# Moving the block for overflowing experts from behind expert 7 to behind expert 60

## The chip, the core and the metric

The kernel runs on one core of a Trainium2 chip: TensorE (PE, with its weight loads PEld), VectorE (DVE), ScalarE (ACT), GpSimd (POOL) and SyncE (SP). Each engine takes its own instructions in order; they wait for each other through semaphores. Transfers between the chip's memory and on-chip memory run on the core's 16 DMA engines and are issued from the queue of an engine, here nearly all from SP. The metric is device microseconds of one execution; times are the median of several executions. A profile is of one execution, and its span goes from the first to the last instruction.

## The reference, cut to what matters

The input is 256 tokens of width 1024, with 16 learned tokens in front. One layer of two linear-attention mixers (gated DeltaNet and GLA) is followed by a mixture of experts, and the result is normalised:

```
h   = h + hybrid_mixer(rmsnorm(h, norm_mix), ...)
xn  = rmsnorm(h, norm_ffn)
group  = argmax(xn @ w_group + b_group)                  # 8 groups
e1, e2 = top 2 of the 8 experts inside the group         # 64 experts in all
y[t]   = sum over e1, e2 of gate * ((silu(xn @ w1[e]) * (xn @ w3[e])) @ w2[e])
out = rmsnorm(h + y, norm_final)                         # the 16 learned tokens are dropped
```

An expert has w1 and w3 (1024 x 512) and w2 (512 x 1024) in float32, 6.3 MB. Which tokens go to which expert is known only at run time; 512 token places fall on 64 experts.

## The kernel before, in words

The mixer takes the first 400 us or so. Behind it all 64 experts are worked through in order, whatever their number of tokens. An expert has room for 32 tokens (`CAP`). What does not fit is done by a block that runs a loop over lists of overflowing experts, with a number of turns that is known only at run time; this is the function `overflow` (L1370). It reads the number of turns into a register of every engine, and a `tc.If` (L1372) jumps over the loop where it is zero.

**Weights.** The host lays the weights out as `wx[e, part]`: parts 0 and 1 hold w1 and w3 of one half of the 1024 rows each, part 2 holds w2. A part is 2 MB and stands in one buffer of 16 KB per partition: `lateA` to `lateE` and `ring0` to `ring4`. `ring_load` (L172) issues a part from SP's queue (L193); expert 63's parts go as two halves of 1 MB. `ring_more` (L195) issues as many as there are free buffers; `ring_take` (L204) hands a part out for use and puts its buffer back on the free list, and the load of the next part into it waits until PE has read the old one. Each transfer reports on one of eight completion semaphores, which the framework gives out in turn, whatever queue the transfer is issued from; a transfer is issued only when the one before it on the same semaphore has landed.

**One expert** (the loop from L1425 on). `up` (L1313) multiplies the expert's gathered tokens `xg` with parts 0 and 1 into the PSUM bank `h13` (matmuls `h`, 64 of them in the trace). `swiglu` (L1325) makes `sl` on ACT and `hid` on DVE, `turn` (L1332) transposes it on PE and copies it to `hT`, and `down` (L1348) multiplies it with part 2 into the banks `y0` and `y1` (matmuls `y`, 16). `scaled` (L1343) writes the two halves of the result to `ys`: ACT the first 512 columns, DVE the second. `back` (L1367) adds `ys` to the tokens' rows by one-hot matmuls into four PSUM banks `acc` that stay open over all experts (matmuls `acc`, 8). In the program text an expert's `back` stands in the next expert's turn, behind that one's `up` and `swiglu`; the framework's scheduler, which simulates the times of each stretch between branches, sets the order on each engine's queue.

**The tile that holds `ys`.** From expert 4 on `ys` lies in `yy[0]`, a tile of 2048 columns: even experts use the first 1024, odd ones the second (`scratch`, L1358). The block's loop uses the same tile: its 16 transfers of w1 and w3 and its 4 of w2 go from SP into the two halves of `yy[0]` in turn (L1402 to L1416), and its own `ys` into the first half.

```
wo = yy[0][:, 1024 * (k % 2):][:, :1024]                       # in overflow, k from 0 to 7
return [yy[0][:, 1024 * (e % 2) + 512 * i:][:, :512] for i in range(2)]   # scratch(e)
```

**The end.** Behind expert 62 the residual `h` is added to `acc` by 8 matmuls with the identity, and `norm_final` is loaded into the same tile that held `h` (L1482). Expert 63's `down` works by halves; then come the sum of squares, the reciprocal root on POOL, the scaling on DVE and four stores.

`with after(slab_dma)` keeps a load of experts' weights behind the last load of the mixer's weights on SP's queue; it may only name an instruction of the same stretch between branches.

Of the kernel before, what the change touches and what calls it, by code (L numbers as in the profile page):

```python
# [18 lines left out]
P = 128  # L19
D = 1024  # L20
# [6 lines left out]
NE = 64  # L27
# [69 lines left out]
def _body(tc, a, dbg, stop, ctx, nc, V, S, G, PE):  # L97
# [7 lines left out]
    def ts(out, in0, s1, s2, op0, op1=None, eng=None, **kw):  # L105
        e = eng or V
        if op1 is None:
            e.tensor_scalar(out, in0, s1, None, op0=op0, **kw)  # L108
        else:
            e.tensor_scalar(out, in0, s1, s2, op0=op0, op1=op1, **kw)  # L110

    def tt(out, in0, in1, op, eng=None):
        return (eng or V).tensor_tensor(out, in0, in1, op)  # L113
# [10 lines left out]
    def mm(out, lhsT, rhs, start=True, stop=True, **kw):  # L124
        return PE.matmul(out, lhsT, rhs, start=start, stop=stop, **kw)  # L125
# [35 lines left out]
    nload, slab_dma, gathered, gather_after, lead, x_act, x_dve = [0], [None], [None], [None], [None], [None], [None]  # L161

    def after(cell):

        return tc.issue_after(cell[0].ins) if cell[0] is not None else ExitStack()
# [6 lines left out]
    def ring_load(n, count):  # L172

        e, part, hf = n // 6, n // 2 % 3, n % 2
        if e == SPARE // 6:
            part = (0, 2, 1)[part]
        if n == SPARE:
            ring[e, part] = [w2p.tile([P, 2048], F32, name="ys", bufs=1)]
        elif hf == 0 or n == SPARE + 1:
            slot = ring_free.pop(0)  # L180
            ring.setdefault((e, part), []).extend((slot[0].tile([P, 4096], F32, name=slot[1], bufs=1), slot))
        t = ring[e, part][-2 if n != SPARE else 0]
        src = wx[e, part]
        if n == SPARE:
            to, src = t, src[:, 0:2048]
        elif part == 2 and e == NE - 1:
            hs = slice(512 * hf, 512 * hf + 512)
            to, src = t.rearrange("p (j d) -> p j d", j=4)[:, :, hs], src.rearrange("p (j d) -> p j d", j=4)[:, :, hs]
        else:
            hs = slice(2048 * hf, 2048 * (hf + count))  # L190
            to, src = t[:, hs], src[:, hs]
        with after(slab_dma):
            nc.sync.dma_start(to, src)  # L193

    def ring_more(n=6 * NE, whole=True):  # L195
        while n and nload[0] < 6 * NE and (ring_free or (nload[0] % 2 == 1) != (nload[0] == SPARE + 1) or nload[0] == SPARE):
            i = nload[0]
            count = 2 if whole and i % 2 == 0 and i != SPARE and i < 6 * (NE - 1) else 1
            ring_load(i, count)
            nload[0] += count  # L200
            n -= 1

    def ring_take(e, part):
        *spare, t, slot = ring.pop((e, part))  # L204
        ring_free.append(slot)
        return (spare[0], t) if spare else t
# [936 lines left out]
    def rt(shape, name):  # L1143
        return mo.tile(shape, F32, name=name)
# [93 lines left out]
    def overflow_list():  # L1238
        ec, eo = rt([P, 2, 64], "ec"), rt([P, 2, 64], "eo")
        tt(ec, rp, C2("ecode")[:, None, :].to_broadcast([P, 2, 64]), ALU.add)  # L1240
        for i, cd in enumerate((cd1, cd2)):
            tt(eo, oh12[:, :, i], ec, ALU.mult)
            V.tensor_reduce(cd, eo, axis=AX.X, op=ALU.add)
        over = rt([P, 64, 7], "over")
        tt(over, cnt[:, :, None].to_broadcast([P, 64, 7]), C2("steps")[:, None, :].to_broadcast([P, 64, 7]), ALU.is_gt)
        nit = rt([P, 1], "nit")
        V.tensor_reduce(nit, over.rearrange("p a b -> p (a b)"), axis=AX.X, op=ALU.add)
        V.tensor_copy(niti, nit)
        ov = over.rearrange("p a b -> p (a b)")
        tt(ov, ov, C2("icode"), ALU.mult)  # L1250
        V.max(items[:, 0:8], ov)
        V.match_replace(out=ov, in_to_replace=items[:, 0:8], in_values=ov, imm_value=0.0)
        V.max(items[:, 8:16], ov)
        ts(items, items, 1.0, 1.0, ALU.max, ALU.subtract)
        V.tensor_copy(itemi, items)
        ts(itemi, itemi, 3, None, ALU.arith_shift_right)
        ts(items, items, 32.0, None, ALU.mult)
# [5 lines left out]
    def bank(*names):  # L1263
        return [pm.tile([P, 512], F32, name=n) for n in names]
# [18 lines left out]
    def group(g):  # L1283

        es = slice(GR * g, GR * g + GR)
        ohs = w2p.tile([P, 2, GR * CAP], F32, name="ohs")
        orep = w2p.tile([P, 2, GR, P], F32, name="orep", bufs=1)
        with after(gathered):
            for t in range(2):
                late_dve[0] = tt(ohs[:, t].rearrange("p (e s) -> p e s", e=GR), rp[:, t, es][:, :, None].to_broadcast([P, GR, CAP]),  # L1290
                   slots[:, None, :CAP].to_broadcast([P, GR, CAP]), ALU.is_equal)
        XG[g] = w2p.tile([P, KT, GR * CAP], F32, name="xg")
        yield from gather(XG[g], ohs, GR * CAP, *((2, ("y0", "y1", "misc", "y0")) if g == 0 else ()))
        with after(gathered):
            for t in range(2):
                tt(orep[:, t], rp[:, t, es][:, :, None].to_broadcast([P, GR, P]), slots[:, None, :].to_broadcast([P, GR, P]), ALU.is_equal)
        p = pm.tile([P, 512], F32, name="misc")
        for e in range(GR):
            for t in range(2):
                mm(p[:, 2 * e:2 * e + 2], orep[:, t, e], rg[:, t, GR * g + e], start=(t == 0), stop=(t == 1))  # L1300
        SC[g] = w2p.tile([P, GR, 2], F32, name="sc")
        V.tensor_copy(SC[g], p[:, 0:2 * GR].rearrange("p (e c) -> p e c", c=2))
        yield
        for e0 in range(0, GR, 2):
            p = pm.tile([P, 512], F32, name="misc")
            for e in range(2):
                for t in range(2):
                    PE.transpose(p[:, (2 * e + t) * P:(2 * e + t + 1) * P], orep[:, t, e0 + e], ident)
            WOT[g, e0] = w2p.tile([P, 2, 2, P], F32, name="wot", bufs=4)
            act(WOT[g, e0], p.rearrange("p (e t x) -> p e t x", e=2, t=2))  # L1310
            yield
# [53 lines left out]
    def back(out, wot, ys, start, stop):  # L1365
        for t in range(2):
            for hf in range(2):  # L1367
                mm(out[2 * t + hf], wot[:, t], ys[hf], start=start, stop=stop)
# [73 lines left out]
    for e in range(NE):  # L1442
        g, i = divmod(e, GR)
        if i == 0 and e:
            for _ in nxt:
                pass
            nxt = group(g + 1) if g + 1 < NE // GR else iter(())
        a0, a1 = ring_take(e, 0), ring_take(e, 1)
        with after(lead if e == 1 else [None]):
            ph = up(XG[g], (a0, a1), slice(CAP * i, CAP * i + CAP), bank("acc3" if e == 1 else "h13")[0],  # L1450
                    {0: first_group, NE - 1: keep_warm}.get(e))
        hid = swiglu(ph, SC[g][:, i])
        if e == 0:
            nxt = group(1)
        if e == 1:
            acc = bank("acc0", "acc1", "acc2", "acc3")
        if last is not None:
            back(acc, *last, start=(e == 1), stop=False)
        hT = turn(hid)
        for _ in range(2):  # L1460
            next(nxt, None)
        c0 = ring_take(e, 2)
        if e == NE - 1:
            break
        ys = down(hT, c0, SC[g][:, i], scratch(e))
        last = (WOT[g, i // 2 * 2][:, i % 2], ys)
        if e == 1:
            with tc.issue_after(late_dve[0].ins):
                overflow_list()
        if e == OVER:  # L1470
            back(acc, *last, start=False, stop=False)
            last = None
            slab_dma[0] = None
            overflow(acc)
            gathered[0] = None
        ring_more()
        if e == NE - 2:
            for t in range(2):
                for hf in range(2):
                    mm(acc[2 * t + hf], ident, h[:, t, hf * 512:hf * 512 + 512], start=False, stop=False)  # L1480
            nfin = keep.tile([P, 2, D], F32, name="h")[:, 0]
            nc.sync.dma_start(nfin, a["norm_final"][None, :].to_broadcast([P, D]))  # L1482


    py, sc, wot = bank("y0", "misc", "y1", "h13"), SC[g][:, i], WOT[g, i // 2 * 2][:, i % 2]
# [36 lines left out]


GR = 4
OVER = 7
SPARE = 20
WARM = 72
E1 = 0
# [74 lines left out]
```

## Time and profile before

| | us |
|---|---|
| median of 3 runs | 1344.37 (1342.24 to 1346.36) |
| the profiled execution | 1344.17 |
| its span | 1342.4 |
| PE busy | 1179.6 (88% of the span) |
| DVE, ACT, POOL busy | 447.5, 314.6, 92.4 |
| transfers of queue q1 (SP's) | 457.43 MB, 83.4% of 16 engines' span |

The span is 24165 instructions long; it is cut in 40 slices of 33.6 us in the page's second part. A busy share is an average over the mixer, where PE is the busiest, and the experts, where the transfers are.

### The profile page before, as it was taken

Reading aid. Unit: us, or ns where it says so; the run is one execution under the profiler, and the core shown is the slowest. Engines: PE = TensorE matmul, PEld = TensorE weight load, DVE = VectorE, ACT = ScalarE, POOL = GpSimd, SP = SyncE. Lnnn points to the kernel's source line nnn. Section 1 sums busy time; section 2 is a strip of 40 time slices with the busy share of each in tenths; the row PEclk is TensorE's granted clock in tenths of the full one; section 3 lists DMA queues with packets and bytes.
Section 4 is the critical chain, followed back from the end, with each engine's and each line's share of the span. In section 5 each row is a group of like instructions: output and inputs, shape, how many; then the busy total and the mean of one; then the engine's idle time right before and its main releaser. Section 6 shows DMA issues by size and latency. Waiting matters only on the chain.

```text
span 1342.4 us, 24165 instructions
## 1 busy us (share of the span) xinstructions
PE 1179.6 (88%) x10513; PEld 760.3 (57%) x10513; DVE 447.5 (33%) x1007; ACT 314.6 (23%) x681; POOL 92.4 (7%) x163
## 2 busy tenths in 40 slices
PE   9999999999999998898878888788788878878776
PEld 8998999899997454344333434334343434334323
DVE  6689787656665222111110101111110111111101
ACT  5575565365441111101000000100000001010101
POOL 1016214502000000000000000000000000000000
PEclk8999999999999999999998898989998998999999
DMA  7633332333997999899999999999999999999995
GB/s 267 217 111 110 113 117 90 126 110 117 369 372 306 427 428 426 366 427 427 427 426 428 428 427 426 426 429 427 425 428 429 427 425 428 428 428 425 428 425 226
DMA packets 46287, 459.53 MB, mean 342 GB/s; under 512 B 5441, under 2 KB 5697, under 8 KB 20450
## 3 DMA queue, kind: packets, MB, share of 16 engines
q1 hardware_dynamic: 45890, 457.43, 83.4%
q8 instruction: 83, 1.36, 0.4%
q10 hardware_dynamic: 288, 0.52, 0.1%
q14 instruction: 26, 0.21, 0.0%
HBM read 456.89 MB, written 1.05 MB: 341 GB/s over the span
## 4 chain that ended last, share of the span: by engine, by line
DMA 44%; PE 15%; ACT 1%; DVE 1%; issue 0%; DVEq 0%; POOL 0%; SPq 0%
DMA ring<-wx 15%; DMA lateB<-wx 9%; DMA lateA<-wx 9%; DMA lateE<-wx 6%; PE acc L125 5%; PE h L125 4%; DMA lateC<-wx 3%; DMA lateD<-wx 3%; PE y L125 3%; PE misc L125 2%; ACT ys L116 1%; ACT sl L116 0%; DVE hid L1329 0%; PE misc L1334 0%; DVE hT L1336 0%
## 5 line engine op out<-in xcount | busy, mean ns | idle before, releaser
L125 PE MATMUL acc<-ys,wot 128*128 128x512 f32 x480 | 226.8, 615 | 27.6 <-ACT ys L116 26.9
L125 PEld LDWEIGHTS acc<-ys,wot 128*128 128x128 f32 x480 | 88.6, 195 | 155.6 <-issue 92.3
L1329 DVE SCALAR_TENSOR_TENSOR hid<-h,sc,sl 128x128 f32<-128x128 f32 x63 | 22.1, 350 | 451.6 <-ACT sl L116 451.6
L125 PE MATMUL ip<-xh,lateD 128*128 128x256 f32 (+2 forms) x784 | 162.3, 297 | 0.0
L116 ACT ACTIVATE sl<-h,sc 128x128 f32<-128x128 f32 x63 | 23.2, 368 | 481.5 <-PE h L125 476.1
L125 PE MATMUL h<-ring,xg 128*32 128x256 f32 x2048 | 124.9, 382 | 6.5 <-DMA ring<-wx 6.3
L125 PEld LDWEIGHTS ip<-xh,lateD 128*128 128x128 f32 x784 | 128.8, 194 | 1.9 <-issue 0.3
L125 PE MATMUL ip<-xl,lateD 128*128 128x256 f32 (+2 forms) x392 | 115.6, 295 | 0.0
L116 ACT ACTIVATE ys<-y,sc 128x512 f32<-128x512 f32 (+1 forms) x61 | 41.5, 680 | 280.4 <-PE y L125 280.4
L125 PEld LDWEIGHTS h<-ring,xg 128*32 128x32 f32 x2048 | 62.5, 110 | 74.7 <-issue 25.6
L108 DVE TENSOR_SCALAR ys<-y,sc 128x512 f32<-128x512 f32 x59 | 44.3, 750 | 167.7 <-PE y L125 167.7
L113 DVE TENSOR_TENSOR lateD<-slab,lateD 128x1024 fp32r<-128x1024 f32 x64 | 80.9, 1264 | 30.7 <-ACT lateD L116 29.4
L116 ACT ACTIVATE lateD<-slab 128x1024 fp32r<-128x1024 f32 x64 | 67.7, 1058 | 57.0 <-PE ip L125 54.7
L125 PE MATMUL y<-ring,hT 128*32 128x512 f32 x496 | 68.2, 667 | 14.4 <-DMA ring<-wx 14.0
L125 PEld LDWEIGHTS ip<-xl,lateD 128*128 128x128 f32 x392 | 75.8, 194 | 1.1 <-issue 0.3
L125 PEld LDWEIGHTS misc<-ohs,h 128*128 128x128 f32 x488 | 56.8, 191 | 22.2 <-issue 12.1
L125 PE MATMUL misc<-ohs,h 128*128 128x128 f32 x488 | 62.7, 281 | 6.4 <-DVE hT L1336 6.4
L156 POOL TENSOR_TENSOR rss<-rss,c 128x1 f32<-128x1 f32 x2 | 1.1, 556 | 925.2 <-DVE rss L103 925.2
L1334 PE MATMUL misc<-c,hid 128*128 128x128 f32 x64 | 20.8, 324 | 49.0 <-DVE hid L1329 49.0
L125 PE MATMUL ip<-xl,wh 128*128 128x256 f32 (+2 forms) x192 | 57.3, 298 | 0.0
L125 PE MATMUL ip<-xh,wh 128*128 128x256 f32 (+2 forms) x192 | 56.8, 296 | 0.0
L125 PE MATMUL ip<-xh,wl 128*128 128x256 f32 (+2 forms) x192 | 56.1, 292 | 0.0
(480 smaller groups left out, 1643.0 us busy)
## 6 DMA issues: line engine op xcount, KB each, us to landing
ring<-wx SPq DMA_DIRECT2D x90, 2048.0 KB, 39.2
lateA<-wx SPq DMA_DIRECT2D x19, 2048.0 KB, 39.2
lateD<-wx SPq DMA_DIRECT2D x19, 2048.0 KB, 39.2
slab<-w_in SPq DMA_DIRECT2D x72, 512.0 KB, 3.7
lateC<-wx SPq DMA_DIRECT2D x18, 2048.0 KB, 39.2
lateB<-wx SPq DMA_DIRECT2D x18, 2048.0 KB, 39.2
lateE<-wx SPq DMA_DIRECT2D x17, 2048.0 KB, 39.1
ring<-wx SPq DMA_DIRECT2D x12, 1024.0 KB, 8.9
```

What stands on the lines that cost most here:

```text
L108: e.tensor_scalar(out, in0, s1, None, op0=op0, **kw)
L113: return (eng or V).tensor_tensor(out, in0, in1, op)
L116: return S.activation(out, in_, func, **kw)
L125: return PE.matmul(out, lhsT, rhs, start=start, stop=stop, **kw)
L156: G.tensor_tensor(out, x, C(name, n)[:, :w], ALU.pow)
L1329: late_dve[0] = V.scalar_tensor_tensor(hid, ph[:, P:256], sc[:, 0:1], sl, op0=ALU.mult, op1=ALU.mult)
L1334: PE.transpose(p[:, 0:P], hid, ident)
```

## The change

The block is called behind expert 60 and no longer behind expert 7. `ring_more` is called ahead of it, so that at expert 60 all 384 halves are issued before it, and an assertion says so. `slab_dma` is cleared behind every expert and not only where the block stands, and the load of `norm_final` is issued from ACT's queue (`S`) and not from SP's.

```diff
+        ring_more()
         if e == OVER:
+            assert nload[0] == 6 * NE
             back(acc, *last, start=False, stop=False)
             last = None
-            slab_dma[0] = None
             overflow(acc)
             gathered[0] = None
-        ring_more()
+        slab_dma[0] = None
         if e == NE - 2:
             for t in range(2):
                 for hf in range(2):
                     mm(acc[2 * t + hf], ident, h[:, t, hf * 512:hf * 512 + 512], start=False, stop=False)
             nfin = keep.tile([P, 2, D], F32, name="h")[:, 0]
-            nc.sync.dma_start(nfin, a["norm_final"][None, :].to_broadcast([P, D]))
+            S.dma_start(nfin, a["norm_final"][None, :].to_broadcast([P, D]))
...
-OVER = 7
+OVER = 60
```

## Rows read from the trace of the kernel before

**Rows 1.** The page's second part: GB/s in 40 slices of the span.

```profile
GB/s 267 217 111 110 113 117 90 126 110 117 369 372 306 427 428 426 366 427 427 427 426 428 428 427 426 426 429 427 425 428 429 427 425 428 428 428 425 428 425 226
```

**Rows 2.** The page's fourth part: the chain of waits, shares of the span by engine.

```profile
DMA 44%; PE 15%; ACT 1%; DVE 1%; issue 0%; DVEq 0%; POOL 0%; SPq 0%
```

**Rows 3.** Windows: us, engines' busy time (instructions), granted clock, DMA share, GB/s.

```profile
540.00:545.00 5.00, 4.76 (x37) 2.89 (x38) 0.92 (x2) 1.18 (x2) 0.00 (x0) 1.00 0.37 98
545.00:550.00 5.00, 5.00 (x44) 2.34 (x46) 0.00 (x0) 0.00 (x0) 0.00 (x0) 1.00 0.86 357
```

**Rows 4.** Waits of SP's queue: us in total, times, longest.

```profile
SPq L193 <- DMA ring<-wx: 339.9, 75, 5.9
...
SPq L1372 <- SPq L1372: 28.7, 7, 6.2
```

**Rows 5.** Line 1372 on SP, whole span and 538 to 544: ns, first and last start.

```profile
L1372 SPq EVENT_SEMAPHORE  x9: 17/17/17, 515.0 to 543.4; - x9
...
L1372 SPq EVENT_SEMAPHORE  x2: 17/17/17, 543.3 to 543.4; - x2
```

**Rows 6.** Timeline, 519 to 545 us: start, us, engine, line [idle before <- releaser].

```profile
519.04 1.93 PE L125 MATMUL h<-lateC,xg 128*32 128x256 f32 x32 [0.41 <-PEq L1372]
...
541.71 1.94 PE L125 MATMUL y<-ring,hT 128*32 128x512 f32 x16
...
543.54 0.34 SPq L193 DMA_DIRECT2D lateC<-wx  x1
...
543.74 0.69 ACT L116 ACTIVATE ys<-y,sc 128x512 f32<-128x512 f32 x1 [5.05 <-PE y L125]
543.78 0.75 DVE L108 TENSOR_SCALAR ys<-y,sc 128x512 f32<-128x512 f32 x1 [1.79 <-PE y L125]
```

**Rows 7.** Timeline of SP's queue, 1258 to 1310 us: the last loads.

```profile
1258.59 0.33 SPq L193 DMA_DIRECT2D lateB<-wx  x1
1263.47 0.33 SPq L193 DMA_DIRECT2D ring<-wx  x1
...
1278.13 16.16 SPq L193 DMA_DIRECT2D ring<-wx  x4
1298.90 10.31 SPq L193 DMA_DIRECT2D lateE<-wx  x2
1309.32 1.84 SPq L1482 DMA_DIRECT2D h<-norm_final  x1
```

**Rows 8.** Tile lateE, 1290 to 1342 us: its loads' starts, and issue to landing.

```profile
L193 SPq DMA_DIRECT2D lateE<-wx x2: 655/3061/5467, 1298.9 to 1303.7; - x2
...
DMA to landing us min/median/max: 25.1/26.2/27.3
```

**Rows 9.** Timeline, 1298 to 1313 us: expert 61's end and expert 62.

```profile
1298.97 1.95 PE L125 MATMUL y<-lateB,hT 128*32 128x512 f32 x16 [1.85 <-DMA lateB<-wx]
1301.02 0.75 DVE L108 TENSOR_SCALAR ys<-y,sc 128x512 f32<-128x512 f32 x1 [3.57 <-PE y L125]
1301.04 0.69 ACT L116 ACTIVATE ys<-y,sc 128x512 f32<-128x512 f32 x1 [4.68 <-PE y L125]
1301.78 1.99 PE L125 MATMUL acc<-ys,wot 128*128 128x512 f32 x4 [0.86 <-ACT ys L116]
...
1308.85 1.93 PE L125 MATMUL h<-ring,xg 128*32 128x256 f32 x32
...
1312.57 0.37 ACT L116 ACTIVATE sl<-h,sc 128x128 f32<-128x128 f32 x1 [10.85 <-PE h L125]
```

**Rows 10.** Windows, 1284 to 1286 us.

```profile
1284.00:1286.00 2.00, 1.70 (x9) 0.52 (x13) 0.00 (x0) 0.00 (x0) 0.00 (x0) 0.50 0.96 410
```

**Rows 11.** Timeline of PE at expert 60's last product.

```profile
1284.30 3.35 PE L125 MATMUL y<-ring,hT 128*32 128x512 f32 x16 [3.06 <-DMA ring<-wx]
```

**Rows 12.** Windows, 15 to 20 us.

```profile
15.00:20.00 5.00, 5.00 (x22) 4.63 (x21) 3.35 (x5) 2.38 (x3) 2.50 (x3) 0.50 0.84 293
```

## Prediction

> **What bounds the kernel now.** I read the page's second part first, for where the transfers are at their ceiling. From the fourteenth slice on the kernel moves 425 to 429 GB/s in every slice but two: one at 366, which runs from 537 to 570 us, and the last [rows 1]. So from about 435 us the experts go at the pace at which 64 × 6.3 MB of weights arrive, one 2 MB load in 4.9 us, 14.7 us for an expert. The chain of waits agrees: 44% of the span is DMA, 15% PE, nearly nothing else [rows 2]. Its PE pieces between 519 and 655 us only say that a freed buffer let a load be issued; the queue was never empty there after 550. Time is therefore won where the queue runs dry before the end, or where the tail behind the last loads gets shorter.
>
> The slice at 366 is the place of the block. Cut in 5 us stretches, it shows 98 and then 357 GB/s between 540 and 550 us [rows 3]. The waits of SP's queue name the line: L1372, the `If`, 28.7 us in 7 waits, the longest 6.2 [rows 4]. Its nine semaphore instructions run from 515.0 to 543.4 us, the last two at 543.3 and 543.4 [rows 5], and the next load leaves SP at 543.54 [rows 6]. The reader is to see what the block costs when it is not taken (no instruction of its body is in the trace). Transfers report on eight completion semaphores in turn. The path that skips the body must raise each of them by what the body's 20 transfers would have added, and SP does that one after the other, waiting before each for the load under way on that semaphore. So SP stands until everything issued has landed, and no load is behind it.
>
> **The change part by part.** *The block leaves expert 7.* SP goes on issuing. The loads lost there: (427−98)/427 × 5 + (427−357)/427 × 5 = 3.85 + 0.82 = 4.7 us; from the slice, (427−366)/427 × 33.6 = 4.8. I take 4.8, bounds 4.5 and 5. At 515 us some six loads were still under way (28.3 us of waits at 4.9 each), and the three that expert 7's freed buffers allow would have joined them, so without the block the queue does not run dry, and every later landing comes 4.8 us earlier.
>
> *The block arrives behind expert 60.* By then SP has issued all loads, so nothing of theirs stands behind the wait. What stands behind it is less visible. The body loads its weights into `yy[0]`, the two halves in turn, and behind the block ACT and DVE write their scaled results `ys` into the same tile: odd experts into the second half. These copies must wait for the body's last transfers into their part of it, that is for semaphores that on the skipped path SP raises. The body's 15th and 16th transfers (w1 and w3 of k=7) went to the second half's two quarters; with eight semaphores in turn they fall on those of the second last and the very last load issued ahead of the block. In the program of the kernel before, ACT's copy of expert 9 waits for the first, DVE's for the second, and both for that of the 20th. There it was hidden: the last load's semaphore was raised at 543.3 [rows 5], and expert 9's `y` matmuls, begun at 541.71, ended only at 543.65; the copies started at 543.74 and 543.78 [rows 6]. The cover was 0.4 us.
>
> At expert 60 it is gone. The first expert behind the block is 61, odd. Its copies now start at 1301.04 and 1301.02 [rows 9], 4.8 us earlier without the gap: 1296.2. But the last loads ahead of the block are then the halves of expert 63's w2. SP issues 8 loads ahead: each leaves as the one eight before it lands (1258.59, 1263.47, and so on) [rows 7]. The two halves (tile lateE) leave at 1298.9 and 1303.7 and land 27.3 and 25.1 us later [rows 8], at 1326.2 and 1328.8; this way round, because the other would land the second at 1331.0 behind norm_final, which was issued after it on that queue. Less 4.8: 1321.4 and 1324.0. So ACT's copy of expert 61 can start at 1321.4 and not at 1296.2.
>
> *What that holds up.* On ACT the later `sl` and `ys`; on PE, whose queue is in order, the `acc` matmuls of expert 61, and behind them all of 62 and 63. PE's path from there now has no DMA wait in it: `acc` of 61 with the residual begins at 1301.78, expert 62 at 1308.85, and the span ends at 1342.4 [rows 9], so 40.6 us from that `acc` to the end. The copy takes 0.69 [rows 9], with 0.1 around it: `acc` begins at 1322.2. Its first eight matmuls use ACT's half and last 3.5 us, so that DVE's half (1324.0 + 0.75 + 0.1 = 1324.9) is there in time.
>
> *The clock behind the wait.* PE stands 26 us. Before expert 60's `y` it stood 3.06 us, and the sixteen matmuls took 3.35 us [rows 11] where expert 61's took 1.95 [rows 9]: 1.4 us lost, with a granted clock of 0.50 [rows 10], the lower level, 1.2 GHz. At the start of the kernel the half clock lasted longer, still 0.50 from 15 to 20 us [rows 12]. Bounds: 0, and 5 us (some 10 us at half pace, an estimate from that start). I take 1.5, by the nearest row.
>
> *The branch itself.* At expert 7 PE lost 0.41 us in front of the first `h` matmul [rows 6]. Behind expert 60 this lies ahead of a wait of 25 us: nothing either way.
>
> *norm_final from ACT.* It must follow the residual's matmuls, which read the tile that it overwrites; they come after the wait, when no load is left. SP needed 1.84 us for this issue [rows 7]; on ACT that lies beside 3.7 us of PE between the residual and `sl`. Nothing; 1.8 if that cover fails. Moving `ring_more` and clearing `slab_dma` change the order of no load that I can name: nothing, bounds ±0.5.
>
> *Sum.* 1322.2 + 40.6 + 1.5 = 1364.3 us of span; 1.8 us lie around the span in the profiled execution (1344.17 against 1342.4): **1366 us**. Against that execution it is −4.8 + 25.2 + 1.5 = +21.9, where 25.2 is the distance from 1296.2 to 1321.4. The median of the runs, 1344.37, is 0.2 above it, so the figure holds for the median too.
>
> **Rivals.** *A: the order on PE is another.* If the matmuls of expert 62 are queued ahead of expert 61's `acc`, they run inside the wait: 3.7 us and about 1 of `sl` and `hid` drop out of the tail, 1361. For it: the program text has them in that order. Against it: in all late experts the queue has `acc` first, and the landing of weights that this order reckons with does not change. 0.13.
>
> *B: only the last transfer into the half counts.* The copies then wait for the 20th transfer's semaphore alone, the fourth in SP's turn, on which the second half of expert 63's first load lands. Four 4.9 us loads behind the one that expert 61's `y` waited for until 1298.97 [rows 9], that is 1318.5, less 4.8: 1313.7. `acc` at 1314.5, + 40.6 + 1.5 + 1.8: 1358. Against it: the wait on the other two is in the program before. 0.05.
>
> *C: the copies do not wait; norm_final does.* Then `acc` of 61 begins 4.8 us early, but norm_final's issue sits in ACT's queue ahead of expert 62's `sl` and needs the fifth semaphore, free only after SP has raised it at about 1316.5, where `sl` is due at 1312.57 − 4.8 = 1307.8 [rows 9]; with its own 1.84 us ACT is free 10.5 us late: 1344.2 − 4.8 + 10.5 = 1350. On SP the trace shows such holding: 339.9 us of SP's waits are for a load to land before the next is issued [rows 4]. The Trainium skill, "DMA: Bandwidth & Descriptors", section "Anatomy of one DMA", says that DMA engines do not wait on semaphores and any such wait happens on the issuing sequencer before dispatch; by that rule moving the transfer to ACT moves its wait into ACT's in-order queue, and SP's rows here agree. 0.04.
>
> *D: faster.* Neither wait is there, or both are met: the body's writes count as done for every engine that did not run it. Then only the gap goes: 1344.2 − 4.8 = 1339.4, and the branch's 0.4 us fall into the 1.85 us for which PE waits at expert 61's `y` [rows 9]. It decides at the copies of expert 61: if they start near 1296, it is this. For it: in the trace before no copy is held. Against it: that those were held for 0.4 us less than they needed anyway. 0.07.
>
> That the block costs SP nothing where it leaves (no gain) is excluded by the two stretches at 98 and 357 GB/s.
>
> **How the numbers follow.** The forecast's own case has 0.71: 1362 to 1371, from the bounds of the clock (0 to 5) and of the gap. With A it holds 0.84. The range 1358 to 1371 takes in A and the edge of B; C, D and most of B are left out. Faster by over 0.3%: D, 0.07. Within 0.3% (about 4 us, what repeated runs of this kernel can tell from no change): 0.02, a C that is half covered. Slower: 0.91.
>
> **What would show it.** Right: no slice below 420 GB/s between 450 and 1300 us; all `L1372` semaphore instructions of SP between about 1299 and 1324, 4.9 and then 2.5 us apart; `ys` of expert 61 on ACT at about 1321 and on DVE at about 1324, with some 25 us of idle PE before its `acc`; a half clock for a few us behind it; 40 to 43 us from that `acc` to the end. Wrong: copies at about 1296 (D, or C if `sl` of 62 is late behind the DMA issue on ACT), a load that still waits in SP behind the branch, or `h` matmuls of expert 62 inside the wait (A).

## The result, and the profile after

The changed kernel takes 1363.22 us (median of 5 runs, 1362.15 to 1364.38), the kernel before 1342.24 over its five: ratio 1.0166, 95% interval 1.0138 to 1.0194. It is slower by 21 us by the two medians and by 22 us by the ratio. The profiled execution took 1363.22 us with a span of 1360.4.

The transfers did gain. This is the page's second part of the changed kernel, GB/s in 40 slices of 34.0 us; the slice at 366 of [rows 1] is gone, nothing between the 14th and the 38th slice is below 424, and the last two slices hold 258 and 47: the last load lands 41 us ahead of the end.

```profile
GB/s 276 205 122 110 119 104 120 111 109 187 379 315 374 428 427 426 426 429 425 428 426 428 428 425 429 425 428 428 424 428 427 426 428 426 428 426 427 426 258 47
```

The two stretches of [rows 3], in windows of the changed kernel (us, busy time and count of PE, PEld, DVE, ACT, POOL, granted clock, DMA share, GB/s):

```profile
540.00:545.00 5.00, 4.10 (x66) 2.12 (x65) 0.35 (x1) 0.37 (x1) 0.00 (x0) 1.00 1.00 424
545.00:550.00 5.00, 3.76 (x23) 1.57 (x24) 1.04 (x2) 1.28 (x2) 0.00 (x0) 1.00 1.00 419
```

What that won is lost behind expert 60. The waits between 1290 us and the end (engine and line, what was waited for: us in total, times, longest) have two rows that the kernel before has not:

```profile
DVE ys L108 <- SPq L1372: 25.9, 1, 25.9
...
ACT ys L116 <- SPq L1372: 24.4, 1, 24.4
...
PE acc L125 <- ACT ys L116: 22.6, 2, 21.8
```

Line 1372 in the changed kernel, all engines (count: ns min/median/max, first and last start):

```profile
L1372 SPq EVENT_SEMAPHORE  x9: 17/17/17, 1300.5 to 1319.4; - x9
...
L1372 PEldq COMPARE_BRANCH  x1: 6508/6508/6508, 1278.7 to 1278.7; - x1
```

And the timeline from expert 60's `acc` to expert 62's `sl` (start, us, engine, line, tiles, idle before and what ended it), against [rows 9]:

```profile
1278.01 3.70 PE L125 MATMUL acc<-ys,wot 128*128 128x512 f32 x8 [0.82 <-ACTq L1372]
1285.58 3.64 PE L125 MATMUL h<-ring,xg 128*32 128x256 f32 x32 [3.88 <-PEq L1372]
...
1293.69 2.18 PE L125 MATMUL y<-lateB,hT 128*32 128x512 f32 x16 [0.43 <-issue]
1316.91 0.69 ACT L116 ACTIVATE ys<-y,sc 128x512 f32<-128x512 f32 x1 [24.42 <-SPq L1372]
1317.65 3.78 PE L125 MATMUL acc<-ys,wot 128*128 128x512 f32 x4 [21.77 <-ACT ys L116]
1319.53 0.75 DVE L108 TENSOR_SCALAR ys<-y,sc 128x512 f32<-128x512 f32 x1 [25.94 <-SPq L1372]
...
1326.89 1.93 PE L125 MATMUL h<-ring,xg 128*32 128x256 f32 x32
1327.00 0.38 ACTq L1483 DMA_DIRECT2D h<-norm_final  x1
...
1330.67 0.37 ACT L116 ACTIVATE sl<-h,sc 128x128 f32<-128x128 f32 x1 [13.07 <-PE h L125]
```

Expert 61's `y` ends at 1295.87. The copies start at 1316.91 and 1319.53, each 0.1 us behind one of SP's last two semaphore instructions (1316.8 and 1319.4). Line 1372 on SP from 1315 to 1320 us, and the tile lateE, whose two loads are the last:

```profile
L1372 SPq EVENT_SEMAPHORE  x2: 17/17/17, 1316.8 to 1319.4; - x2
```

```profile
L193 SPq DMA_DIRECT2D lateE<-wx x2: 662/3090/5519, 1289.6 to 1294.5; - x2
...
DMA to landing us min/median/max: 24.9/26.0/27.2
```

1289.6 + 27.2 = 1316.8 and 1294.5 + 24.9 = 1319.4. Between the end of `y` and the first `acc` at 1317.65 PE stood 21.8 us.

The chain of waits no longer helps here: it follows a wait back to an instruction that did work, and a semaphore that SP raises is none, so it stops at the copy and sums to 2% PE:

```profile
PE 2%; DVE 0%; ACT 0%; issue 0%; DVEq 0%; POOL 0%; ACTq 0%
```

**Taking the executions apart.** Single executions of one kernel differ by up to 13 us here (1331.66 to 1344.71 for own_tile), and the profiles show that some of it arises before the experts: the first load of experts' weights left at 337.06 us in the profile before and at 331.97 in this one. The granted clock of TensorE goes with it, taken over the first 330 us: the rows of the kernel before, of the changed kernel and of `fill_longer` below, whose first load left at 338.47, in this order:

```profile
0.00:330.00 330.00, 321.44 (x3061) 300.95 (x3062) 242.66 (x560) 186.48 (x445) 89.88 (x159) 0.97 0.43 138
```

```profile
0.00:330.00 330.00, 321.24 (x3104) 301.02 (x3105) 244.97 (x566) 188.44 (x449) 90.61 (x160) 0.99 0.44 140
```

```profile
0.00:330.00 330.00, 322.81 (x3049) 302.06 (x3050) 242.25 (x559) 184.94 (x441) 87.86 (x159) 0.96 0.44 138
```

So each profile is cut at two SP issues, the first load of experts' weights and the first half of expert 63's w2 (lateE, [rows 7]); the two stretches behind the first cut are what the kernels can differ in:

| kernel | ratio to before (95%) | first load, us | first load to lateE | lateE to the end |
|---|---|---|---|---|
| before | | 337.06 | 961.8 | 43.5 |
| changed | 1.0166 (1.0138 to 1.0194) | 331.97 | 957.7 | 70.8 |
| own_tile | 0.9975 (0.9955 to 0.9996) | 330.00 | 958.0 | 43.6 |
| other_half | 1.0090 (1.0059 to 1.0121) | 330.36 | 957.9 | 60.7 |
| no_block | 0.9973 (0.9957 to 0.9990) | 331.63 | 958.1 | 43.3 |
| early_wait | 0.9983 (0.9961 to 1.0005) | 335.48 | 961.3 | 44.8 |
| norm_from_sp | one execution | 333.19 | 957.9 | 71.1 |
| fill_wait | 1.0154 (1.0121 to 1.0186) | 329.78 | 958.0 | 66.3 |
| fill_longer | 1.0108 (1.0073 to 1.0143) | 338.47 | 957.7 | 64.0 |

The change is −4.1 in the first stretch and +27.3 in the second: +23.2 us. The spans of these two executions differ by only 18.0, because the changed one reached its first load 5.1 us earlier; the medians, 21.0 apart, lie between. Each stretch is from one execution of a kernel, but the first one agrees closely: 957.7 to 958.1 us in the seven kernels without the block behind expert 7, 961.3 and 961.8 in the two with it.

### The profile page after: what moved, and what is told of

The parts are those of the page before. It is cut to its first block, busy times and chain, and to the rows that moved or that the text cites. A ratio compares the mean times of both kernels' runs of the same rounds, so it can differ in the third digit from the quotient of the medians.

```text
span 1360.4 us, 24163 instructions
## 1 busy us (share of the span) xinstructions
PE 1186.3 (87%) x10513; PEld 762.3 (56%) x10513; DVE 447.1 (33%) x1007; ACT 314.3 (23%) x681; POOL 92.4 (7%) x163
## 5 line engine op out<-in xcount | busy, mean ns | idle before, releaser
L125 PE MATMUL acc<-ys,wot 128*128 128x512 f32 x480 | 231.5, 626 | 47.0 <-ACT ys L116 45.5
L125 PE MATMUL h<-ring,xg 128*32 128x256 f32 x2048 | 126.9, 386 | 10.1 <-DMA ring<-wx 6.0
L113 DVE TENSOR_TENSOR lateD<-slab,lateD 128x1024 fp32r<-128x1024 f32 x64 | 80.8, 1263 | 28.8 <-ACT lateD L116 27.2
L125 PEld LDWEIGHTS misc<-ohs,h 128*128 128x128 f32 x488 | 56.8, 191 | 22.6 <-issue 12.1
```

## The experiments

**own_tile: the copies write a tile that the block does not load into.**

```diff
-        if e <= SPARE // 6:
+        if e <= SPARE // 6 or e > OVER:
             return [rtp.tile([P, 512], F32, name="hT", bufs=2) for _ in range(2)]
```

> The changed kernel with one difference: the experts behind the block keep their scaled results in tiles of their own, which the block's body does not load into. Theory (the copies of expert 61 wait for semaphores that SP raises when the last loads have landed, because they write the tile of the body's transfers): the copies start right behind the y matmuls, near 1296 us in the changed kernel's time and not at 1316.9 and 1319.5; SP's semaphore instructions still run until about 1319; the acc matmuls start 21 us earlier and 2 us of slow clock go: 1340 us, 1338 to 1343. Rival 1 (the block itself costs it at this place: the branch, or SP standing, whatever tile the copies write): unchanged, 1363. Rival 2 (norm_final's issue on ACT takes over the wait and holds sl of expert 62): sl is late by up to 9 us, 1349.

Measured: 1337.53 us (12 runs) against 1340.39 (30 runs). Timeline and line 1372 of this kernel:

```profile
1288.03 2.24 PE L125 MATMUL y<-lateB,hT 128*32 128x512 f32 x16 [0.52 <-DMA lateB<-wx]
1290.33 0.69 ACT L116 ACTIVATE hT<-y,sc 128x512 f32<-128x512 f32 x1 [3.59 <-PE y L125]
1290.37 0.75 DVE L108 TENSOR_SCALAR hT<-y,sc 128x512 f32<-128x512 f32 x1 [2.54 <-PE y L125]
1291.06 1.98 PE L125 MATMUL acc<-hT,wot 128*128 128x512 f32 x4 [0.80 <-ACT hT L116]
...
1299.07 0.38 ACTq L1483 DMA_DIRECT2D h<-norm_final  x1
...
1301.90 0.37 ACT L116 ACTIVATE sl<-h,sc 128x128 f32<-128x128 f32 x1 [10.89 <-PE h L125]
```

```profile
L1372 SPq EVENT_SEMAPHORE  x9: 17/17/17, 1298.9 to 1319.0; - x9
```

SP raises its semaphores as late as in the changed kernel, and no copy waits: they start with the end of `y`, and from lateE to the end 27 us come back. The loss is the tile that the body's transfers would write, not the place of the block. To share a tile with the body is not enough: the `hT` of the pool `rtp`, which these copies now write, is also the name of the tiles in which the body would build its one-hot matrices, with DVE and without a transfer, and that holds nobody here. Rival 2 falls as well: ACT issues norm_final at 1299.07, and `sl` of expert 62 follows its `h` at 1301.90, held by PE alone. The branch is not in the way either: PE still waits 0.52 us for expert 61's weights behind it. This kernel is faster than both, by 0.25% than the one before, with an interval that just excludes no change; the first stretch of the table gives 3.8 us. The forecast of 1338 to 1343 was missed by 0.5 us on the low side; in this series the kernel before is itself 1.9 us faster than in the one above (1340.39 against 1342.24). The earlier `ring_more`, the cleared `slab_dma` and norm_final from ACT are all in this kernel, and its two stretches are those of no_block to within 0.3 us: together they cost nothing.

**other_half: the halves exchanged for the experts behind the block.**

```diff
-        return [yy[0][:, 1024 * (e % 2) + 512 * i:][:, :512] for i in range(2)]
+        return [yy[0][:, 1024 * ((e + (e > OVER)) % 2) + 512 * i:][:, :512] for i in range(2)]
```

> The changed kernel with the two halves of the tile exchanged for the experts behind the block: expert 61 writes the first half, 62 the second. Theory: the last transfer of the body into the first half is its 19th, on the third semaphore in SP's turn, raised at about 1306.8 us; both copies of expert 61 start there, 10 us earlier than ACT's in the changed kernel; expert 62's copies, which now wait for the last two (1316.8 and 1319.4), are due at about 1324 and wait no longer. 1353 us, 1351 to 1355. Rival 1 (the copies wait until SP is through the block, whatever the semaphore): unchanged, 1363. Rival 2 (any copy into this tile is free if it is not the second half): 1340.

Measured: 1351.70 us; from lateE to the end 10.1 us less than the changed kernel. Its timeline, experts 61 and 62:

```profile
1305.50 0.69 ACT L116 ACTIVATE ys<-y,sc 128x512 f32<-128x512 f32 x1 [19.35 <-SPq L1372]
1305.52 0.75 DVE L108 TENSOR_SCALAR ys<-y,sc 128x512 f32<-128x512 f32 x1 [18.27 <-SPq L1372]
...
1322.85 0.69 ACT L116 ACTIVATE ys<-y,sc 128x512 f32<-128x512 f32 x1 [3.18 <-PE y L125]
1322.89 0.75 DVE L108 TENSOR_SCALAR ys<-y,sc 128x512 f32<-128x512 f32 x1 [2.12 <-PE y L125]
```

SP's semaphore instructions of line 1372 from 1303 to 1306 us:

```profile
L1372 SPq EVENT_SEMAPHORE  x2: 17/17/17, 1303.0 to 1305.4; - x2
```

Both copies now start 0.1 us behind the one at 1305.4, 12.7 us ahead of SP's last (1318.2 in this execution), and expert 62's, which belong to the last two, wait for PE alone. So each copy waits for the semaphore of the transfer that would have written its columns, and not until SP is through.

**no_block: the kernel before without the block** (the loop for overflowing experts is left out).

```diff
-OVER = 7
+OVER = NE
```

> The kernel before without the block (the loop for overflowing experts is left out; with this input it makes no turn). Theory (behind expert 7 the block costs the 4.8 us in which the transfers run dry, and nothing else that reaches the end): no slice below 420 GB/s between 450 and 1290 us, and 0.9964 of the kernel before, 1337.5 us for a median of 1342.2. Rival (the end is set by PE's path from 519 to 655 us, which the chain of waits lists, and the gap was filled anyway): the same as before, 1342.

Measured: ratio 0.9973; first load to lateE 958.1 us against 961.8, lateE to the end 43.3 against 43.5. Its GB/s by slice:

```profile
GB/s 276 211 121 117 114 111 96 128 112 126 373 349 340 427 428 426 428 426 427 427 427 427 427 426 427 429 427 428 426 427 428 427 426 427 427 427 427 428 426 211
```

The gap was on the path, and the PE pieces that the chain lists between 519 and 655 us were not. At the last load it is worth 3.7 us here, 4.1 in the changed kernel, and not the 4.8 that the rates give. The rates themselves are right: in the 50 us from 200 us behind the first load on, which hold the gap, the kernel before moved 387 GB/s and the changed one 426, which is 39/426 × 50 = 4.6 us.

```profile
537.06:587.06 50.00, 42.97 (x380) 21.24 (x376) 8.73 (x19) 5.30 (x10) 0.00 (x0) 1.00 0.93 387
```

```profile
531.97:581.97 50.00, 44.47 (x401) 21.50 (x400) 8.08 (x17) 5.04 (x9) 0.00 (x0) 0.97 1.00 426
```

**early_wait: the same wait behind expert 7.** The kernel before, block behind expert 7, with the same edit, so that expert 8 has to wait for the last two semaphores.

```diff
-        return [yy[0][:, 1024 * (e % 2) + 512 * i:][:, :512] for i in range(2)]
+        return [yy[0][:, 1024 * ((e + (e > OVER)) % 2) + 512 * i:][:, :512] for i in range(2)]
```

> The kernel before, block behind expert 7, with the halves exchanged for the experts behind it: expert 8 writes the second half, and its copies have to wait for the last two semaphores, raised at about 543.3 us, where they were due at 529.4. Theory: the same wait as in the changed kernel, 14 us, stands in the trace, but PE has over 50 experts in which each of its turns is 1.5 us or more shorter than three loads, and catches up before the end; the transfers keep enough free buffers: the same time as before within 0.3%. Rival (a wait of this kind costs its length wherever it stands): 14 us slower, 1356.

Measured: ratio 0.9983, no difference. Timeline of this kernel, a later window, and its PE at expert 61's last product:

```profile
536.20 0.69 ACT L116 ACTIVATE ys<-y,sc 128x512 f32<-128x512 f32 x1 [13.24 <-SPq L1372]
...
536.94 3.78 PE L125 MATMUL acc<-ys,wot 128*128 128x512 f32 x4 [6.92 <-ACT ys L116]
...
541.10 0.75 DVE L108 TENSOR_SCALAR ys<-y,sc 128x512 f32<-128x512 f32 x1 [14.20 <-SPq L1372]
```

```profile
560.00:600.00 40.00, 34.47 (x308) 16.77 (x306) 7.17 (x15) 3.76 (x7) 0.00 (x0) 1.00 1.01 428
```

```profile
1296.80 3.30 PE L125 MATMUL y<-lateB,hT 128*32 128x512 f32 x16 [1.85 <-DMA lateB<-wx]
```

Waits of 13.2 and 14.2 us stand in the trace, of which PE stands 6.9 us in front of `acc`, and they cost nothing that the interval shows: the loads are back at 428 GB/s by 560 us, and PE has caught up over the 55 experts that follow, since at expert 61 it waits 1.85 us for weights as in [rows 9]. The 1.3 us by which this execution is longer behind lateE are this `y`, for the most part at the lower clock level (0.57 from 1297 to 1300 us): 3.30 us and not 1.95. Behind expert 60 there is nothing left to catch up in.

**norm_from_sp: the last part of the change undone.**

```diff
-            S.dma_start(nfin, a["norm_final"][None, :].to_broadcast([P, D]))
+            nc.sync.dma_start(nfin, a["norm_final"][None, :].to_broadcast([P, D]))
```

> The changed kernel with norm_final issued from SP's queue again, behind the raising of the semaphores. Theory (this part of the change is worth nothing): it leaves SP at about 1327 us behind the residual's matmuls, lands 25 us before it is needed at 1354; 1363 us, from 1360 to 1366. Rival (it was moved because SP issues it too late): the scaling at the end waits for it, and the span is longer by the time from 1354 to its landing.

Measured: 1364.0 us in one execution, 71.1 us from lateE to the end against 70.8. SP issues it here:

```profile
1328.88 0.35 SPq L1483 DMA_DIRECT2D h<-norm_final  x1
```

It lands 3.7 us later, 23.5 us before the first scaling at 1356.12. This part is worth nothing, as far as one execution shows.

**fill_wait and fill_longer: PE kept busy inside the wait.** `ylast` is the last `y` matmul that was written.

```diff
+        if e == OVER + 1:
+            fill = pm.tile([P, 512], F32, name="misc")
+            with tc.issue_after(ylast[0].ins):
+                for _ in range(320):                # 400 in fill_longer
+                    mm(fill[:, 0:P], zero, zero)
```

> The changed kernel with 320 small matmuls of zeros on PE between expert 61's y and its acc, some 19 us of work that nobody reads, inside the wait. Theory (behind the wait PE runs at half clock for some us because it stood): the acc matmuls and the residual's take 7.1 us to expert 62's first h and not 9.2, at a granted clock of 1.00; the copies start as before at about 1317 and 1319.5; 1361 us, 2 less than the changed kernel. Rival (the slow clock there comes from the branch or from the transfers, not from the standing): 9.2 us again, 1363.

Measured: 1361.17 us. The edit did two things: with the matmuls of zeros in the queue the scheduler put expert 62's `h` ahead of expert 61's `acc`, inside the wait (the order of rival A), and PE then stood 4.3 us before the copies came:

```profile
1315.86 2.08 PE L125 MATMUL acc<-ys,wot 128*128 128x512 f32 x2 [4.28 <-ACT ys L116]
1317.73 0.75 DVE L108 TENSOR_SCALAR ys<-y,sc 128x512 f32<-128x512 f32 x1 [29.92 <-SPq L1372]
...
1318.53 5.49 PE L125 MATMUL acc<-ys,wot 128*128 128x512 f32 x6 [0.60 <-DVE ys L108]
...
1329.87 1.94 PE L125 MATMUL y<-lateD,hT 128*32 128x512 f32 x16
```

From lateE to the end it is 4.5 us shorter than the changed kernel, which is about rival A's price and not the clock's: the granted clock was 0.50 again. So the forecast time of 1361 was met by luck, not by the reason given for it, and this kernel says nothing on its own about the clock; fill_longer was made of it.

> As fill_wait, with 400 matmuls in place of 320, so that PE works up to the moment at which the copies come and does not stand 4.3 us ahead of them. In both, expert 62's h matmuls run inside the wait. Theory (the slow clock behind the wait comes from the standing): from expert 61's first acc to expert 62's y at a granted clock of 1.00 and in some 9 us, the wait for DVE's copy included, and not in 14.0 us as in fill_wait with 0.50 over its first 8; 4 us less than fill_wait, 1357. Rival (the slow clock comes from something else at that place): 14 us again, 1361.

Measured: 1357.20 us. PE worked until ACT's copy was there, and 1.1 us beyond it:

```profile
1323.93 0.69 ACT L116 ACTIVATE ys<-y,sc 128x512 f32<-128x512 f32 x1 [29.53 <-SPq L1372]
...
1325.70 1.13 PE L125 MATMUL acc<-ys,wot 128*128 128x512 f32 x2
1326.54 0.75 DVE L108 TENSOR_SCALAR ys<-y,sc 128x512 f32<-128x512 f32 x1 [30.90 <-SPq L1372]
...
1327.34 2.84 PE L125 MATMUL acc<-ys,wot 128*128 128x512 f32 x6 [0.52 <-DVE ys L108]
...
1335.84 1.94 PE L125 MATMUL y<-lateD,hT 128*32 128x512 f32 x16
```

The same eight `acc` matmuls and the residual's eight up to expert 62's `y`: 10.1 us and not 14.0. The windows behind the copies, of fill_wait and of fill_longer:

```profile
1320.00:1322.00 2.00, 2.00 (x3) 0.67 (x2) 0.00 (x0) 0.00 (x0) 0.00 (x0) 0.50 0.00 0
```

```profile
1328.00:1330.00 2.00, 2.00 (x6) 0.83 (x5) 0.00 (x0) 0.00 (x0) 0.00 (x0) 1.00 0.00 0
```

At 1.2 GHz in the one, at 2.4 in the other. The two kernels differ only by 80 matmuls of zeros, and so in whether PE stood 4.3 us before the copies: the slow clock comes from the standing. Its price is not the whole 3.9 us: 1.0 of it is that in fill_longer PE was still busy with expert 62's `h` when ACT's copy ended (1324.62), so that the stretch begins later against the loads. From DVE's copy, which is tied to the last load in both, to `y` it is 12.1 and 9.3 us: 2.8 us for the clock. Measured from the issue of lateE, DVE's copy comes 0.4 us later in fill_longer (30.4 against 30.0); that leaves 2.4, and the table has 2.3. The medians, 1361.2 and 1357.2, lie further apart, but their intervals overlap (1.0121 to 1.0186 and 1.0073 to 1.0143), so the gain on the whole time is not shown by itself.

## Why the prediction was right, point by point

**The bound and the gap.** Right in kind: the block behind expert 7 held SP until every load had landed, and moving it let the transfers run on. The term was sized at 4.8 us. The rates confirm it where the gap is (4.6), but the issue of the last load came only 3.7 (no_block) to 4.1 us (changed, by the two cuts) earlier. Where the rest goes between the gap and that issue stays open: outside the gap both run at 427 GB/s in every window that I compared.

**The wait that takes its place.** Right, and decided by other_half: the copies of expert 61 wait for the second last and the last load of all, through semaphores that SP raises on the skipped path. Forecast for ACT's copy 1321.4, measured 1316.91, which is 1322.0 if the 5.1 us of the earlier start are put back: 0.6 late, as the gap was worth less.

**What it holds up.** `acc` to the end was forecast as 40.6 + 1.5 = 42.1 us; it was 1360.4 − 1317.65 = 42.75. The 0.65 are the clock: `acc` and the residual took 9.24 us (1317.65 to 1326.89) and not 7.07 [rows 9], 2.2 us for the term put at 1.5. In other_half they took 9.34, and the pair of fill_wait and fill_longer gives 2.8: here the slow clock behind such a wait costs 2.2 to 2.8 us, inside the bounds of 0 and 5.

**The branch.** Without effect, as forecast, and in five of the six kernels with the block behind expert 60 of the size that was taken from expert 7's row [rows 6]: PE stood 0.40 or 0.41 us in front of `h`, although the compare-and-branch took 1.75 to 2.85 us there and not 0.35, because the `acc` matmuls ran beside it. In the changed kernel's execution it took 6.5 us and PE was held 3.88, ahead of a wait that hid it. The cause of these lengths was not sought.

**Rivals.** A did not happen; the queue has `acc` first, as forecast, and fill_wait shows what the other order would have brought, some 4 us. B falls with the two copies starting 2.6 us apart. C was wrong in a detail besides: to judge by own_tile, norm_final's transfer has the first of the eight semaphores and not the fifth. ACT issued it at 1299.07, right behind SP's first semaphore instructions (1298.9) and 0.94 us behind the start of expert 62's `h`, where the changed kernel has 0.11; it was held 0.8 us and not 10. D is what own_tile does, and it gives what was forecast for it in kind: 0.9975, where D said 0.9964.

**The number.** 1366 against 1363.2: −5.1 for the start of this execution, +0.5 gap, +0.7 clock, +1.0 for 2.8 us around the span in place of 1.8. The start has nothing to do with the argument, it is the largest of these terms, and it pulls against the rest: that the number is this close is in part luck. By the two cuts, which leave the start out, +21.9 was forecast and +23.2 measured. The range of the forecast's own case, 1362 to 1371, was also wider than its terms: clock at 0 or 5, gap at 5 or 4.5 and the ±0.5 give 1363.9 to 1370.4, and 1363.2 lies just below that.

## What to carry to other kernels

A block that is never entered is not free: in this framework the path around it has to raise every semaphore that its body would have raised, in order and behind the transfers under way, and whatever writes where the body's transfers would have written waits for that. Where such a wait stands decides what it costs: 14 us cost nothing with 55 experts to follow, 25 us cost all of it, and 2 us of slow clock on top, with two. Before a block is moved to where the issuing queue no longer minds, list the tiles that its transfers write and who writes them next; here a tile that no transfer of the body writes gave the change its gain.

## What was not expected

The compare-and-branch on PE took 6.5 us in one execution, 1.75 to 2.85 us in five others at the same place, and 0.35 us behind expert 7.

The time of the mixer differs by 8.7 us between executions of kernels that are alike there (first load of experts' weights from 329.78 to 338.47 us), and the granted clock of the first 330 us goes with it in all nine profiles: 0.99 in the five with 329.78 to 331.97, 0.98 for 333.19, 0.97 for 335.48 and 337.06, 0.96 for 338.47. The first 25 us alone do not sort them: four of the nine have 0.86 there, with first loads from 331.63 to 338.47. Why the clock differs was not looked into. The 8.7 us are about twice the gain that was looked for, and a reason to cut profiles at a common event before comparing them.
